# Parking all three merge gates in DRAM, running branch C ahead of branch A, and doing every convolution tap on VectorE

## The chip, the cores and the metric

The kernel runs on one core of one Trainium2 chip. The metric is the device time of one execution in microseconds (us), as the median of several runs.

## What is computed

Two decoder layers run over a prompt of 512 tokens and a sample group of 8 sequences with 4 new tokens each, 544 columns together. A layer projects the normalised input once and splits the result among three branches:

```python
u  = a_val * sigmoid(a_glu)                      # branch A: causal depthwise convolution, width 31
ya = silu(layernorm(conv31(u) + b_dw)) * silu(a_gate)
yb = sparse_attention(q, k, v, top-k of relu indexer) * silu(b_gate)   # branch B, prompt and paged cache
o, S = hgrn2(silu(cq), log_f, kk, ci, S0)        # branch C: gated linear recurrence
yc = rmsnorm(o) * silu(c_gate)
m = sigmoid(g_a)*(ya @ w_proj_a) + sigmoid(g_b)*(yb @ w_proj_b) + sigmoid(g_c)*(yc @ w_proj_c)
y = x + gate * (m @ w_out)
```

## The kernel before

Activations lie with channels on the 128 partitions and the 544 columns along the free dimension. Every projection is made of **products** (`product`, L493): one 128-column weight tile against all 544 columns. The weight is split into a rounded part `whi` (ScalarE) and a remainder `wlo` (VectorE, or GpSimd for every third product outside branch B's input), and three matmuls per 128 rows and column half (`whi` with `hhi`, `whi` with `hlo`, `wlo` with `hhi`) sum up in a PSUM tile `wide`, of which there are two. A product over 1024 rows has 48 matmuls of 272 columns, one over 512 rows (`projs`, names `yhi`, `ylo`) has 24. A layer has 73 of the first kind and 24 of the second.

Everything else is spread between the products. `spawn(gen, n, time)` registers a generator of n steps over `time` (a product over 1024 rows counts 5600 of it), `pump` runs due steps after each product, `drain` runs the rest. The program order and the priorities (`at`) feed a scheduler that writes one fixed instruction order for each engine; each engine then works its list in order and waits on semaphores. Loads and stores of one kind go through SyncE's queue (SP), the cache gathers through GpSimd's.

The order of a layer before, in products: branch B's inputs (9; called stage B below), first half of branch A (4, A0), first half of branch C (6, C0), second half of A (4, A1), second half of C (6, C1), the gates `gc` (8), `agate` (4), four times two `ga` gates and two of branch A's output projection (16, of them 8 short), `cgate` (4), C's output projection (8 short, PC), `gb` (8), `bgate` (4), B's output projection (8 short, PB), `w_out` (8). Beside them run:

- `sample_scores` (L921): keys are gathered, transposed (`gI` to `kit`), and 32 matmuls with an output of 32 partitions each (`hold<-kit,qib`) make the scores of one of four chunks. They stand in one block per chunk, 256 matmuls in all.
- `sample_select` (L966): a bit search in 31 steps; in each VectorE counts (`junk`), TensorE sums (`hold<-cnt`), VectorE decides (`rej`, `X`).
- `convolve` (L1205): per 128 channels 31 taps over 512 columns. The first 19 are VectorE's (one `tensor_scalar`, 18 `scalar_tensor_tensor`, `y<-u,wdw,y`, L1234). The other 12 (`CP`) are multiplied on ScalarE (`ctap`) and summed on GpSimd (`cpool`, L1239), and VectorE adds the two sums.
- the heads of branch C (`heads` in `branch_c`, on all engines), and `attends` (L876): prompt index with 16 rounds of `max` and `match_replace` for each of three query blocks (`prompt_masks`), sample attention, prompt attention.

Of the gates, `gc` is stored to DRAM (`gates`) and loaded back into a `th` tile, of which there are three, when C's projection needs it; `ga` goes to `th` tiles just ahead of its use, `gb` to eight tiles in SBUF.

Of the kernel before, what the change touches and what calls it, by code (L numbers as in the profile page):

```python
# [15 lines left out]
KD = D // 128  # L16
# [13 lines left out]
CP = 12  # L30
# [88 lines left out]
class _Kernel:  # L119
# [448 lines left out]
    def run(self):  # L568
# [33 lines left out]
        for l in range(self.depth):  # L602
# [15 lines left out]
            self.open("y")  # L618
            self.open("a", side="right")
# [4 lines left out]
            y = self.t([128, 4, NT], "y", "y")  # L624
            st = {}
            self.branch_a(l, h, V, y, 0, st)
# [5 lines left out]
            self.open("c")  # L632
            yc = self.t([128, 4, NT], "yy", "yc")
            self.branch_c(l, h, V, 0, yc, st)
# [4 lines left out]
            def gate_tile(f):  # L639
                return self.t([128, NT], "th", "w", bufs=3)  # L640
            self.gates("gc", h, gate_tile, then=lambda f, t: self.store(gd[:, f], t))
            self.drain(st["a0"], st["a1"], select)
            self.close("sel", "sidx", "a")
            self.open("split", side="right")
            ys = self.gated(COL["agate"], h, y, 0.5)
            m, mn, ta = [], [], {}

            def half():

                mn.append("m%d" % len(m))  # L650
                self.open(mn[-1], side="right")
                t = self.t([128, KD // 2, NT], "m", mn[-1])
                m.extend(t[:, f] for f in range(KD // 2))
            half()
            self.drain(st["c0"], st["c1"])
            self.close("c")
            half()
            self.open("isc")
            yb = [self.t([128, 4, NT], "y", "y")]
            attend = self.spawn(self.attends(l, r, yb), 75, 120000)  # L660

            def use_a(f, p):
                self.stt(self.two(m[f]), self.two(ta[f]), 1.0, p, OP.add, OP.mult)
            for f in range(0, KD, 2):
                self.gates("ga", h, gate_tile, range(f, f + 2), ta.__setitem__)
                self.projs(l, "w_proj_a", ys, range(f, f + 2), use_a)
            ys = self.gated(COL["cgate"], h, yc, 1.0)

            def use_c(f, p):
                t = self.t([128, NT], "th", "w", bufs=3)  # L670
                self.at(self.clk - 15000)
                self.load(t, gd[:, f], chain=False)
                self.at(self.clk - 16000)
                self.stt(self.two(t), self.two(t), 1.0, p, OP.add, OP.mult)
                self.tt(m[f], m[f], t, OP.add, eng=nc.gpsimd)
            tb = [self.t([128, 4, NT], "yy", "yc")]
            self.projs(l, "w_proj_c", ys, range(KD), use_c)
            self.open("tb")
            tb.append(self.t([128, 4, NT], "tb", "tb"))
            self.gates("gb", h, lambda f: tb[f // 4][:, f % 4])  # L680
# [4 lines left out]
            def use_b(f, p):  # L685
                t = tb[f // 4][:, f % 4]
# [4 lines left out]
            self.close("tb", "isc", "yc", "y", "keep")  # L691
            self.open("x")
            xT, w = self.out_proj(l, mh, xd, mod["g"], more)
            self.close(mn[1], mn[0], "split")
# [59 lines left out]
    def branch_b_in(self, l, h, V):  # L754
# [56 lines left out]
        scores = self.spawn(self.sample_scores(l, r), 9, 22500)  # L811
# [109 lines left out]
    def sample_scores(self, l, r):  # L921
# [9 lines left out]
        for c in range(4):  # L931
            sp = self.hold()
            kt = {}
            for hf in range(2):
                raw = next(raws)
                for rp in range(2):
                    b = self.bank()
                    for x in range(4):
                        self.tr(b[:, x * 128:(x + 1) * 128], raw[x][:, 2 * rp:2 * rp + 2].rearrange("p r d -> p (r d)"))
# [651 lines left out]
```

## Time and profile before

| | |
|---|---|
| median of 3 runs | 1712.63 us (1702.94 to 1713.41) |
| the profiled execution | 1704.63 us, span of its instructions 1702.8 us |
| TensorE matmul busy | 1567.7 us, 92% |
| VectorE, ScalarE, GpSimd busy | 1062.3 us (62%), 712.4 us (42%), 646.4 us (38%) |
| granted TensorE clock, mean | 0.950 |

TensorE is busy nearly all the time, and the share says little on how much of that time was needed: the clock and the idle time differ by stage. The stages of both layers therefore have to be read one by one, with the busy time of the other engines beside TensorE's.

### The profile page before, as it was taken

Reading aid. Unit: us, or ns where it says so; the run is one execution under the profiler, and the core shown is the slowest. Engines: PE = TensorE matmul, PEld = TensorE weight load, DVE = VectorE, ACT = ScalarE, POOL = GpSimd, SP = SyncE. Lnnn points to the kernel's source line nnn. Section 1 sums busy time; section 2 is a strip of 40 time slices with the busy share of each in tenths; the row PEclk is TensorE's granted clock in tenths of the full one; section 3 lists DMA queues with packets and bytes.
Section 4 is the critical chain, followed back from the end, with each engine's and each line's share of the span. In section 5 each row is a group of like instructions: output and inputs, shape, how many; then the busy total and the mean of one; then the engine's idle time right before and its main releaser. Section 6 shows DMA issues by size and latency. Waiting matters only on the chain.

```text
span 1702.8 us, 31340 instructions
## 1 busy us (share of the span) xinstructions
PE 1567.7 (92%) x12580; PEld 1412.2 (83%) x12580; DVE 1062.3 (62%) x2047; ACT 712.4 (42%) x1205; POOL 646.4 (38%) x536
## 2 busy tenths in 40 slices
PE   8889879889999999999988897878999999999998
PEld 5677778789998788998887687878899888799998
DVE  4433898987848474345555149899886485543562
ACT  4345443455354242453233455325633433334432
POOL 0332575574524544110321316674643444431010
PEclk9989989899999999999988898989999999999999
DMA  9653521232354556315725342212323655552131
GB/s 357 217 161 109 199 54 59 75 90 85 107 150 150 153 180 179 88 50 198 267 96 160 92 121 67 73 50 76 103 82 102 187 142 164 169 136 84 50 134 47
DMA packets 95209, 215.49 MB, mean 127 GB/s; under 512 B 11949, under 2 KB 41363, under 8 KB 94024
## 3 DMA queue, kind: packets, MB, share of 16 engines
q1 hardware_dynamic: 81752, 171.53, 32.4%
q0 software_dynamic: 13312, 41.96, 8.3%
q8 instruction: 99, 1.62, 0.4%
q14 instruction: 46, 0.38, 0.1%
HBM read 183.90 MB, written 26.22 MB: 123 GB/s over the span
## 4 chain that ended last, share of the span: by engine, by line
PE 66%; DVE 17%; issue 7%; DMA 4%; ACT 2%; POOL 1%; another core or an unknown queue 1%; SPq 0%; ACTq 0%; DVEq 0%; POOLq 0%
PE wide L197 46%; PE bk L197 8%; DVE y L228 7%; PE hold L197 7%; PE bk L201 5%; DVE wlo L220 2%; DVE hE L220 1%; DMA araw<-in_w_ada 1%; DVE y L225 1%; DVE junk L225 1%; DVE hqa L220 1%; DVE X L228 1%; DMA xraw<-in_constf 1%; DMA wraw<-in_w_in 1%
## 5 line engine op out<-in xcount | busy, mean ns | idle before, releaser
L197 PE MATMUL wide<-hhi,whi 128*128 128x272 f32 (+1 forms) x2336 | 523.6, 302 | 32.1 <-DVE ht L225 9.1
L197 PE MATMUL wide<-hhi,wlo 128*128 128x272 f32 (+1 forms) x2336 | 524.2, 302 | 11.6 <-DVE wlo L220 8.4
L197 PE MATMUL wide<-hlo,whi 128*128 128x272 f32 (+1 forms) x2336 | 524.3, 302 | 1.2 <-issue 1.0
L197 PEld LDWEIGHTS wide<-hhi,whi 128*128 128x128 f32 (+1 forms) x2336 | 387.3, 196 | 47.5 <-issue 32.3
L197 PEld LDWEIGHTS wide<-hhi,wlo 128*128 128x128 f32 (+1 forms) x2336 | 386.8, 196 | 24.4 <-issue 12.9
L197 PEld LDWEIGHTS wide<-hlo,whi 128*128 128x128 f32 (+1 forms) x2336 | 387.0, 196 | 13.6 <-issue 11.0
L209 ACT ACTIVATE whi<-wraw 128x1024 fp32r<-128x1024 f32 (+2 forms) x198 | 183.7, 931 | 315.7 <-PE wide L197 226.9
L220 POOL TENSOR_TENSOR wlo<-wraw,whi 128x1024 fp32r<-128x1024 f32 (+1 forms) x58 | 123.1, 2123 | 447.2 <-ACT whi L209 387.4
L220 DVE TENSOR_TENSOR wlo<-wraw,whi 128x1024 fp32r<-128x1024 f32 (+2 forms) x140 | 160.3, 1146 | 127.8 <-ACT whi L209 101.7
L220 POOL TENSOR_TENSOR cpool<-cpool,ctap 128x512 f32<-128x512 f32 (+1 forms) x94 | 142.1, 1512 | 56.9 <-ACT ctap L209 41.2
L228 DVE SCALAR_TENSOR_TENSOR y<-u,wdw,y 128x512 f32<-128x512 f32 x144 | 159.1, 1118 | 0.4
L916 POOL DMA_INDIRECT gI<-in_cache_idx_k,idx x64 | 64.2, 1003 | 129.9 <-PE bk L201 111.9
L916 POOL DMA_INDIRECT gKV<-in_cache_v,idx x64 | 63.1, 985 | 80.0 <-PE bk L201 32.6
L209 ACT ACTIVATE ctap<-u,wdw 128x512 f32<-128x512 f32 x88 | 62.7, 719 | 69.9 <-POOL cpool L220 69.8
L197 PE MATMUL wide<-yhi,whi 128*128 128x272 f32 x384 | 84.5, 297 | 7.6 <-DVE gate L228 3.2
L916 POOL DMA_INDIRECT gKV<-in_cache_k,idx x64 | 65.3, 1020 | 61.3 <-PE bk L201 28.0
L197 PE MATMUL wide<-yhi,wlo 128*128 128x272 f32 x384 | 82.3, 293 | 0.8 <-issue 0.8
L197 PE MATMUL wide<-ylo,whi 128*128 128x272 f32 x384 | 82.7, 293 | 0.0
L209 ACT ACTIVATE kt<-bk 128x512 f32<-128x512 f32 x80 | 46.4, 596 | 81.5 <-PE hold L197 29.9
L197 PEld LDWEIGHTS wide<-yhi,whi 128*128 128x128 f32 x384 | 61.8, 192 | 12.2 <-ACT whi L209 5.6
L197 PE MATMUL bk<-hqa,hk 128*128 128x64 f32 (+2 forms) x480 | 62.1, 263 | 4.0 <-DVE hqa L220 3.9
L238 DVE CUSTOM_DVE_ANT_0 P<-bk,isc 128x512 f32<-128x512 f32 (+2 forms) x48 | 25.5, 556 | 63.5 <-PE bk L197 63.4
(334 smaller groups left out, 2444.3 us busy)
## 6 DMA issues: line engine op xcount, KB each, us to landing
wraw<-in_w_in SPq DMA_DIRECT2D x128, 512.0 KB
wraw<-in_w_ada SPq DMA_DIRECT2D x32, 512.0 KB
araw<-in_w_ada SPq DMA_DIRECT2D x16, 512.0 KB
wraw<-in_w_out SPq DMA_DIRECT2D x16, 512.0 KB
xpark<-xT SPq DMA_DIRECT2D x4, 1088.0 KB
gates<-th SPq DMA_DIRECT2D x16, 272.0 KB
th<-gates SPq DMA_DIRECT2D x16, 272.0 KB
xT<-xpark SPq DMA_DIRECT2D x4, 1088.0 KB
```

The source lines that it names most:

```text
L197: return self.tick(self.nc.tensor.matmul(out, lhsT, rhs, start=start, stop=stop))
L201: self.tick(self.nc.tensor.transpose(out, in_, self.ident[b:b + n, b:b + n]))
L209: i = self.nc.scalar.activation(out, in_, f, **k)
L220: self.tick((eng or self.nc.vector).tensor_tensor(out, a, b, op=op))
L225: self.tick((eng or self.nc.vector).tensor_scalar(out, a, s1, s2, op0=op0, **k))
L228: self.tick(self.nc.vector.scalar_tensor_tensor(out, a, s, b, op0=op0, op1=op1))
L238: self.tick(getattr(self.nc.vector, f)(*a, **k))
L916: self.tick(self.chain("gather", self.nc.gpsimd.indirect_dma_start(out=raw, out_offset=None, in_=rows, in_offset=bass.IndirectOffsetOnAxis ...
```

## The change

- The gate products move: `gc` directly behind branch B's inputs, `ga` and `gb` behind both halves of A. All three are stored to DRAM and loaded back one tile at a time (`parked`), eight loads in each of the three output projections.
- Branch C (12 products) comes ahead of branch A (8).
- The new order of a layer: B (9), `gc` (8), C0 (6), C1 (6), A0 (4), A1 (4), `ga` (8), `gb` (8), `agate` (4), A's projection (8 short, PA), `cgate` (4), PC (8 short), `bgate` (4), PB (8 short), `w_out` (8).
- The scores of the sample keys are spread over 60000 in place of 22500, and the matmuls of a chunk come in two halves, each one step behind its transposes.
- The convolution is drained after the gates and not before `agate`; attention starts with `ga` and has 175000 in place of 120000.
- All 31 taps are VectorE's but the first, which is ScalarE's; `cpool` and `ctap` go.

```diff
             r, scores = self.branch_b_in(l, h, V)
...
+            def park_gates(name):
+                g = gd[name] = self.tc.dram_tile([128, KD, NT], F32, name="%s%d" % (name, l))
+                self.gates(name, h, lambda f: self.t([128, NT], "th", "w", bufs=3),
+                           then=lambda f, t: self.store(g[:, f], t))
+
+            def parked(name, f):
+                t = self.t([128, NT], "th", "w", bufs=3)
+                self.at(self.clk - 15000)
+                self.load(t, gd[name][:, f], chain=False)
+                self.at(self.clk - 16000)
+                return t
+            park_gates("gc")
             self.drain(scores)
...
             select = self.spawn(self.sample_select(l, r), 36, 70000)
...
             self.branch_c(l, h, V, 0, yc, st)
+            self.branch_c(l, h, V, 1, yc, st)
...
+            self.branch_a(l, h, V, y, 0, st)
             self.branch_a(l, h, V, y, 1, st)
-            self.branch_c(l, h, V, 1, yc, st)
-            gd = self.tc.dram_tile([128, KD, NT], F32, name="gates%d" % l)
...
-            self.drain(st["a0"], st["a1"], select)
+            self.drain(st["c0"], st["c1"], select)
...
+            attend = self.spawn(self.attends(l, r, yb), 75, 175000)
+            park_gates("ga")
+            park_gates("gb")
+            self.drain(st["a0"], st["a1"])
...
             def use_a(f, p):
-                self.stt(self.two(m[f]), self.two(ta[f]), 1.0, p, OP.add, OP.mult)
+                t = parked("ga", f)
+                self.stt(self.two(m[f]), self.two(t), 1.0, p, OP.add, OP.mult)
+            self.projs(l, "w_proj_a", ys, range(KD), use_a)
...
             def use_b(f, p):
-                t = tb[f // 4][:, f % 4]
+                t = parked("gb", f)
                 self.stt(self.two(t), self.two(t), 1.0, p, OP.add, OP.mult)
...
-        scores = self.spawn(self.sample_scores(l, r), 9, 22500)
+        scores = self.spawn(self.sample_scores(l, r), 9, 60000)
...
-        z = self.t([128, NT], "cpool", "a")[:, :TP]
-        self.tsc(yp, u[:, 0:TP], w[:, 0:1], V["bdw"][:, f:f + 1], OP.mult, OP.add)
-        self.act(z, u[:, 31 - CP:31 - CP + TP], AF.Copy, scale=w[:, 31 - CP:32 - CP])
-        for k in range(max(CP - 1, 30 - CP)):
-            if k < 30 - CP:
-                self.stt(yp, u[:, k + 1:k + 1 + TP], w[:, k + 1:k + 2], yp, OP.mult, OP.add)
-            if k < CP - 1:
-                n = 32 - CP + k
-                x = self.t([128, NT], "ctap", "a", bufs=2)[:, :TP]
-                self.act(x, u[:, n:n + TP], AF.Copy, scale=w[:, n:n + 1])
-                self.tt(z, z, x, OP.add, eng=gp)
+        self.act(yp, u[:, 0:TP], AF.Identity, scale=w[:, 0:1], bias=V["bdw"][:, f:f + 1])
+        for k in range(1, 31):
+            self.stt(yp, u[:, k:k + TP], w[:, k:k + 1], yp, OP.mult, OP.add)
             if k % 3 == 2:
                 yield
-        self.tt(yp, yp, z, OP.add)
```

On VectorE, in the second half of branch C in layer 0, taps stood before among the heads' work (`hE`, `hqa`), the select's count (`junk`) and the splits:

```order
L228 SCALAR_TENSOR_TENSOR y<-u,wdw,y 128x512
L225 TENSOR_SCALAR junk,cnt_2017<-isc_s,X 128x544
L220 TENSOR_TENSOR hqa<-hqa,hE_3021 128x8x32
L228 SCALAR_TENSOR_TENSOR y<-u,wdw,y 128x512
L220 TENSOR_TENSOR hE_4030<-hE_4004 128x136
```

Now they stand mostly in the gates `ga` and `gb` of layer 0, among the prompt index (`isc`) and the splits:

```order
L219 TENSOR_TENSOR wlo_456<-wraw,whi_455 128x1024
L227 SCALAR_TENSOR_TENSOR y<-u,wdw,y 128x512 x6
L224 TENSOR_SCALAR isc_4417<-irel,wi 128x256
L227 SCALAR_TENSOR_TENSOR y<-u,wdw,y 128x512 x2
L237 TENSOR_REDUCE y<-cprod 128x16
L234 COPY us<-u 128x8x4
L227 SCALAR_TENSOR_TENSOR isc_4417<-irel,wi,isc_4417 128x256
L219 TENSOR_TENSOR wlo_458<-wraw,whi_457 128x1024
```

The taps moved from the heads of branch C to the start of attention.

On TensorE, in branch B's inputs of layer 0, the first scores of the sample keys (`hold`) were one block before:

```order
L197 MATMUL wide<-hhi,whi_463 128x272 x2
L197 MATMUL wide<-hlo,whi_463 128x272
L197 MATMUL hold<-kit,qib 32x128 x32
L197 MATMUL wide<-hlo,whi_463 128x272
L197 MATMUL wide<-hhi,wlo_464 128x272 x2
```

Now each of them stands between matmuls of a product:

```order
L196 MATMUL hold_919<-kit_910,qib_451 32x128
L196 MATMUL wide_1047<-hlo_363,whi0_455 128x272
L196 MATMUL hold_919<-kit_910,qib_451 32x128
L196 MATMUL wide_1047<-hhi_362,wlo0_456 128x272
L196 MATMUL hold_919<-kit_910,qib_451 32x128
L196 MATMUL wide_1047<-hhi_362,wlo0_456 128x272
L196 MATMUL hold_919<-kit_910,qib_451 32x128
L196 MATMUL wide_1047<-hhi_362,whi0_455 128x272
```

Of the 256 such matmuls of the program 24 were followed at once by one of a product, now 251 are.

On SyncE's queue, around B's projection in layer 0, only weights stood before:

```order
L244 DMA wraw<-in_w_proj_b 128x1024 x2
L244 DMA wraw<-in_w_ada 128x1024 x4
L244 DMA wraw<-in_w_proj_b 128x1024 x2
L244 DMA wraw<-in_w_ada 128x1024 x4
L244 DMA wraw<-in_w_out 128x1024 x2
```

Now the loads of the parked `gb` stand between them:

```order
L243 DMA wraw<-in_w_proj_b 128x1024 x2
L243 DMA th<-gb_5376 128x544 x2
L243 DMA wraw<-in_w_ada 128x1024
L243 DMA th<-gb_5376 128x544
L243 DMA wraw<-in_w_ada 128x1024 x3
L243 DMA wraw<-in_w_proj_b 128x1024
L243 DMA xT<-xpark 128x2176 x2
L243 DMA wraw<-in_w_proj_b 128x1024
```

A load that waits for its `th` tile now stands ahead of weights in the same queue.

## Rows read from the trace of the kernel before

**Rows 1.** The page, part 1: busy time, share of the span, instructions.

```profile
PE 1567.7 (92%) x12580; PEld 1412.2 (83%) x12580; DVE 1062.3 (62%) x2047; ACT 712.4 (42%) x1205; POOL 646.4 (38%) x536
```

**Rows 2.** Windows by stage: layer 0 B, C0 to gc; layer 1 the same.

```profile
core 0: us, PE busy (x) PEld busy (x) DVE busy (x) ACT busy (x) POOL busy (x), PEclk, DMA share, GB/s
30.40:150.30 119.90, 107.63 (x777) 82.68 (x776) 47.52 (x95) 44.32 (x75) 38.83 (x43) 0.91 0.59 197
...
188.00:441.30 253.30, 219.91 (x1611) 209.70 (x1612) 229.77 (x389) 110.86 (x176) 151.23 (x112) 0.91 0.27 81
...
877.80:993.40 115.60, 101.44 (x727) 83.37 (x728) 44.37 (x78) 44.77 (x74) 27.83 (x31) 0.83 0.34 101
...
1023.90:1274.20 250.30, 214.52 (x1596) 204.34 (x1595) 227.12 (x384) 113.76 (x178) 150.61 (x113) 0.92 0.25 73
```

**Rows 3.** Windows, columns as in rows 2: C1, and `ga` with A's projection, layer 0.

```profile
292.00:362.70 70.70, 58.45 (x403) 55.87 (x403) 69.46 (x105) 31.06 (x51) 43.28 (x34) 0.85 0.23 68
...
474.80:595.90 121.10, 115.82 (x1053) 101.93 (x1052) 68.40 (x158) 51.78 (x84) 53.66 (x49) 0.99 0.52 153
```

**Rows 4.** The chain that ended last: start us, length us, what.

```profile
838.53 15.03 PE wide L197 x119
```

**Rows 5.** Groups of instructions: count, busy us, mean ns, idle before, releaser.

```profile
L220 DVE TENSOR_TENSOR wlo<-wraw,whi 128x1024 fp32r<-128x1024 f32 (+2 forms) x140 | 160.3, 1146 | 127.8 <-ACT whi L209 101.7 <-remote 11.6 <-issue 10.5
L228 DVE SCALAR_TENSOR_TENSOR y<-u,wdw,y 128x512 f32<-128x512 f32 x144 | 159.1, 1118 | 0.4
L220 POOL TENSOR_TENSOR cpool<-cpool,ctap 128x512 f32<-128x512 f32 (+1 forms) x94 | 142.1, 1512 | 56.9 <-ACT ctap L209 41.2 <-ACT cpool L209 11.8 <-POOL cpool L220 0.3
...
L197 PE MATMUL bk<-hqa,hk 128*128 128x64 f32 (+2 forms) x480 | 62.1, 263 | 4.0 <-DVE hqa L220 3.9
...
L238 DVE MAX8 m<-isc 128x8 f32<-128x256 f32 (+2 forms) x96 | 53.7, 559 | 2.3
L238 DVE MATCH_REPLACE8 isc<-m,isc 128x256 f32<-128x256 f32 (+2 forms) x96 | 52.1, 542 | 0.0
...
L197 PE MATMUL hold<-kt,qbd 128*32 128x128 f32 x512 | 23.5, 281 | 0.5 <-issue 0.5
```

**Rows 6.** Instructions on tile wdw: count, ns min/median/max, first and last start.

```profile
L228 DVE SCALAR_TENSOR_TENSOR y<-u,wdw,y x144: 733/741/6350, 180.6 to 1199.5; 128x512 f32<-128x512 f32 x144
```

**Rows 7.** Instructions on tile kit: idle before them, us and times, by releaser.

```profile
  issue: 48.0, 72
```

**Rows 8.** Timeline of PE: narrow and wide matmuls by turns, in layer 1.

```profile
932.53 0.59 PE L197 MATMUL wide<-hhi,whi 128*128 128x272 f32 x1
933.05 0.64 PE L197 MATMUL hold<-kit,qib 128*32 128x128 f32 x2
933.62 0.60 PE L197 MATMUL wide<-hlo,whi 128*128 128x272 f32 x1
...
1478.30 0.29 PE L197 MATMUL wide<-yhi,wlo 128*128 128x272 f32 x1
1478.52 0.30 PE L197 MATMUL hold<-gKV,kt 128*32 128x128 f32 x1
1479.25 0.29 PE L197 MATMUL hold<-gKV,kt 128*32 128x128 f32 x1 [0.43 <-issue]
1479.47 0.39 PE L197 MATMUL wide<-yhi,wlo 128*128 128x272 f32 x1
```

**Rows 9.** Windows, columns as in rows 2: PC of layer 0; around the turns of layer 1.

```profile
634.30:670.30 36.00, 31.97 (x271) 29.00 (x270) 13.62 (x21) 8.43 (x15) 18.94 (x16) 0.95 0.72 204
...
925.00:950.00 25.00, 21.01 (x94) 13.76 (x93) 3.55 (x5) 5.57 (x8) 4.31 (x5) 0.66 0.32 102
```

**Rows 10.** Waits of SyncE's queue: waited for, us in total, times, longest us.

```profile
SPq L244 <- POOL m L220: 34.5, 8, 13.5
```

More of the change, by code (lines that the diff above doesn't have):

```diff
@@ L29 @@
 WB = 6
-CP = 12
 HK = 4
@@ L631, in run @@
             self.open("yc")
-            self.open("c")
+            self.open("c", side="right")
             yc = self.t([128, 4, NT], "yy", "yc")
+            st = {}
             self.branch_c(l, h, V, 0, yc, st)
-            self.branch_a(l, h, V, y, 1, st)
-            self.branch_c(l, h, V, 1, yc, st)
-            gd = self.tc.dram_tile([128, KD, NT], F32, name="gates%d" % l)
-            def gate_tile(f):
-                return self.t([128, NT], "th", "w", bufs=3)
-            self.gates("gc", h, gate_tile, then=lambda f, t: self.store(gd[:, f], t))
@@ L656, in run @@
[L656 to L660, printed above, removed]
+            self.branch_c(l, h, V, 1, yc, st)
+            self.open("y")
+            self.open("a")
+            y = self.t([128, 4, NT], "y", "y")
+            self.branch_a(l, h, V, y, 0, st)
+            self.branch_a(l, h, V, y, 1, st)
+            self.drain(st["c0"], st["c1"], select)
+            self.close("c", "sel", "sidx")
@@ L662, in use_a @@
+            m = [t[:, f] for t in ms for f in range(KD // 2)]
             def use_a(f, p):
-                self.stt(self.two(m[f]), self.two(ta[f]), 1.0, p, OP.add, OP.mult)
-            for f in range(0, KD, 2):
-                self.gates("ga", h, gate_tile, range(f, f + 2), ta.__setitem__)
-                self.projs(l, "w_proj_a", ys, range(f, f + 2), use_a)
+                t = parked("ga", f)
+                self.stt(self.two(m[f]), self.two(t), 1.0, p, OP.add, OP.mult)
+            self.projs(l, "w_proj_a", ys, range(KD), use_a)
@@ L667, in run @@
             ys = self.gated(COL["cgate"], h, yc, 1.0)
             def use_c(f, p):
[L670 to L673, printed above, removed]
+                t = parked("gc", f)
                 self.stt(self.two(t), self.two(t), 1.0, p, OP.add, OP.mult)
                 self.tt(m[f], m[f], t, OP.add, eng=nc.gpsimd)
-            tb = [self.t([128, 4, NT], "yy", "yc")]
@@ L930, in sample_scores, with part @@
         raws = self.ahead(gathers())
[L931 to L939, printed above, removed]
-                    kt[rp, hf] = self.t([128, 4, 128], "kit", "sg", bufs=4)
-                    self.cp(kt[rp, hf], b.rearrange("p (x k) -> p x k", x=4))
-                yield
+        def part(c, hf, kt, sp):
             for r4 in range(4):
@@ L945, in sample_scores @@
                 for b2 in range(2):
-                    for pr in range(4):
+                    for pr in (2 * hf, 2 * hf + 1):
                         self.mm(sp[32 * pr:32 * pr + 32, k], qib[:, r4 % 2, 2 * pr + b2],
-                                kt[r4 // 2, pr // 2][:, 2 * (pr % 2) + b2], start=b2 == 0, stop=b2 == 1)
+                                kt[r4 // 2][:, 2 * (pr % 2) + b2], start=b2 == 0, stop=b2 == 1)
+            if hf == 0:
+                return
             R = self.t([128, 512], "irel_s", "sg", bufs=2)
@@ L954, in sample_scores @@
             self.cp(sc[s, :512], b[s])
+        last = None
+        for c in range(4):
+            for hf in range(2):
+                raw = next(raws)
+                kt = []
+                for rp in range(2):
+                    b = self.bank()
+                    for x in range(4):
+                        self.tr(b[:, x * 128:(x + 1) * 128], raw[x][:, 2 * rp:2 * rp + 2].rearrange("p r d -> p (r d)"))
+                    kt.append(self.t([128, 4, 128], "kit", "sg", bufs=4))
+                    self.cp(kt[rp], b.rearrange("p (x k) -> p x k", x=4))
+                if last:
+                    part(*last)
+                if hf == 0:
+                    sp = self.hold()
+                last = (c, hf, kt, sp)
+                yield
+        part(*last)
         b = self.bank()
@@ L1284, in heads @@
                 yield
-        st["c%d" % h2] = self.spawn(heads(), 14, (40000 if h2 == 0 else 44000))
+        st["c%d" % h2] = self.spawn(heads(), 14, (34000 if h2 == 0 else 44000))
     def head_in(self, n, hh, st, p, V):
```

47 lines of the change are left out of this document (18 added, 29 removed).

## Prediction

> **What bounds the kernel now.** I read the page's busy shares first, then the stages by windows, then the groups of instructions in the stage that loses most. TensorE is busy for 92% of the span [rows 1], but busy time contains slow clock and matmuls that wait inside, so I measure each stage against what its matmuls need. A wide matmul in an undisturbed run starts every 15.03 / 119 = 0.126 us [rows 4], so a product of 48 needs 6.05 us. For the other matmuls I take 0.09 us a record, between the 62.1 / 480 = 0.13 of `bk<-hqa,hk` and the 23.5 / 512 = 0.05 of `hold<-kt,qbd` [rows 5]; this is an estimate.
>
> From C0 to `gc` there are 28 products, 169.3 us. The windows count 1611 and 1596 records there [rows 2]; 1344 are the products', so 267 and 252 others cost 24 and 23 us. The need is 193 and 192 us, the stages last 253.3 and 250.3: 60 and 58 us are lost in the two layers. In the same rows VectorE is busy for 229.8 and 227.1 us, 91%, and in C1 for 69.46 of 70.70 us [rows 3], where TensorE's granted clock has a mean of 0.85. So VectorE sets the pace of these stages and TensorE waits, partly idle, partly at its lower level. Elsewhere VectorE is not the limit: in `ga` with A's projection it is busy for 68.4 of 121.1 us, TensorE for 115.8 [rows 3].
>
> What fills VectorE there is taps: 144 at a mean of 1118 ns, though the median is 741 and the longest 6350 [rows 5, 6]. GpSimd's `cpool`, 94 times 1512 ns [rows 5], runs in the same stretches; the gap between mean and median is the price of that company.
>
> **The change part by part.** Sums are made against the profiled execution, 1704.6 us (span 1702.8). The median of the three runs is 1712.6, 0.5% above it; about 1% is what a measurement of this kernel can tell from no change.
>
> *Branch C's stages lose their taps.* In the new order `gc`, C0 and C1 hold 165 VectorE instructions in layer 0 and no tap. Before, the 389 instructions of C0 to `gc` [rows 2] had 72 taps, 80 us; the rest averages 150 / 317 = 0.47 us, so 165 cost 78 us. TensorE needs 20 x 6.05 = 121 us for the products and, with 304 other matmuls of two records each, 55 us: 176 us, more than twice VectorE's. The 118 us lost before should go: **-118**; with the other records at 0.13 or 0.05 it is -96 or -141. I leave in these stages what a stage with a slack VectorE still loses, 5.3 of 121.1 us or 4.4% [rows 3], on 2 x 176 us: **+15**.
>
> *The taps go to A0, A1, `ga`, `gb`.* All 30 per group are VectorE's now, 240 in place of 144. Per layer 120 taps at 0.77 us make 92 us. I take 0.77 since `cpool` is gone and the quiet tap is 0.741; the far end is 1.118 [rows 5, 6]. Then 16 splits at 1.146 = 18 us; 26 (layer 0) and 31 (layer 1) pairs of `max` and `match_replace` at 0.559 + 0.542 = 29 and 34 us [rows 5]; and 160 other instructions. Without taps, splits and pairs VectorE has 637 us in 1571 instructions [rows 1, 5], 0.41 us each, so 65 us. The sum is 204 and 210 us. TensorE needs 24 x 6.05 = 145 us and, for 348 and 388 other matmuls of two records, 63 and 70: 208 and 215. The two engines are level, and level is not free. If VectorE reaches the 91% of rows 2, the stages last 225 and 231 us: 17 and 16 us lost, **+33**. The lower bound is the 4.4% of a slack stage, +18; the upper has taps at 1.118, which adds 42 us of VectorE per layer, gives 271 and 278 us, and loses 126.
>
> ScalarE loses 88 multiplications and GpSimd 88 sums. Both are worth nothing by themselves (42% and 38% busy, rows 1); their worth is the tap's price, counted above.
>
> *Parked gates.* `ga` and `gb` add 32 stores and 32 loads. The stores follow a gate product that nothing waits for, beside other work: 0. The loads stand on SP's queue ahead of weights, and each waits until one of three `th` tiles is free. Before, SP waited for GpSimd's sum `m` in exactly these loads of `gc`, 8 times and 34.5 us in all, 13.5 at the longest [rows 10]. What of it reached TensorE is seen in PC of layer 0: 36.0 us, of which 8 short products need 192 x 0.126 = 24.2 and 79 others 7.1 [rows 9]; 4.7 us lost, 0.6 per load. In PA and PB no `m` sum on GpSimd holds the tile, VectorE frees it directly, so I take half, 0.3 x 32 = **+10** (0 to +19). Queued behind a waiting load are weights of PA, PB, PC and `w_ada`; they are needed some products later.
>
> *Key scores.* Their 256 matmuls of 32 output partitions stood in blocks of 32, and their tile lists 48.0 us of idle with no releaser, in 72 pieces [rows 7]; at 0.05 us a record the work itself is another 23 us, 71 in all. Now 251 of them stand singly between wide matmuls. At full clock the step wide to narrow takes 0.22 us (1478.30 to 1478.52) and narrow to wide 0.22 (1479.25 to 1479.47) [rows 8]. A pair is 0.44 in place of 0.126, 0.31 more: 251 x 0.31 = 78 us. The spread pays about as much as it gets back: 0, with bounds of -30 (these stages also ran at 0.91 and 0.83 of the clock, rows 2) and +25. The Trainium skill, "TensorEngine Tiling (Array Packing)", speaks against this edit: it says that a change of tiling mode drains TensorE. The two steps of 0.22 us in place of 0.126 agree. By that rule alone, with 470 more changes of tile size at 0.09 us and nothing of the idle given back, the sum would end 44 us higher, at 1689.
>
> The other moves (attention started earlier, A's inputs later, `u` tiles from two to four) have their instructions in the counts above.
>
> **Sum:** 1704.6 - 118 + 15 + 33 + 10 = 1645 us, and its own range by the bounds above, without the far end of the taps, 1605 to 1685.
>
> **The rivals.**
>
> (1) *Slower: taps stay at 1.118 us.* Splits, `hk`, `cprod` and gathers are still GpSimd's and can keep VectorE company in A0 to `gb`. Then the excess is 126 and not 33: 1738 us. It passes 1705 when a tap takes about 1.0 us. Against it: GpSimd's busy time falls by over 130 us with `cpool`, and the median was 741 ns even before. Chance 6%. The page "SBUF — State Buffer" of the Trainium skill, "Who interferes with whom", has the mechanism: a VectorE instruction with two SBUF inputs and a GpSimd instruction that reads SBUF exclude each other for a whole instruction.
>
> (2) *Slower: turns of narrow and wide at the lower clock.* Around 925 to 950 us of before such turns ran at a granted clock of 0.66 [rows 9], and a pair took 1.09 us (932.53 to 933.62, rows 8), at the 1.2 GHz level. If all 251 do so, 251 x 0.65 = +163: 1808 us. From 92 pairs on the kernel is slower. For it: in the new order few matmuls of these stages stand in long rows of one size. Against: the old stretch was also starved, with 21.0 of 25.0 us busy in 94 records. Chance 8%.
>
> (3) *No change: the heads' own chain, not VectorE's load, costs C0 and C1.* C1 of layer 0 needs 36.3 + 115 x 0.09 = 46.7 us and lasts 70.7 [rows 3]: 24 lost, in C0 by the same count about 22, so 92 in both layers would stay. 1704.6 - 118 + 92 + 33 + 10 = 1722 us. Against it: VectorE had 1.2 us of idle in C1, and `bk<-hqa,hk` waited for `hqa` for only 4.0 us [rows 5]. Chance 11%.
>
> (4) *Better: level is free after all.* With deep enough spreading the excess of 33 and the rest of 15 vanish: 1597 us. Chance 13%.
>
> **How the numbers follow.** The forecast has 62%, the rivals 6, 8, 11 and 13. The range goes from 1600 to 1710: it holds the forecast's own, half of (4) and a share of (3), and leaves out (1), (2) and most of the rest. Faster by over 1%: the forecast without a small upper tail, and (4), 74%. Within 1%: (3) and that tail, 15%. Slower: (1), (2) and the upper part of (3), 11%.
>
> **What the profile after would show.** Right: the tap's mean falls from 1118 to about 770; from `gc` to C1 TensorE is near 176 us per layer at full clock; A0 to `gb` is some 225 to 230 us with VectorE at 90%; the three short projections lose about 0.3 us per load; the idle before `hold<-kit,qib` shrinks, while its pairs take 0.44 us. Wrong: taps over 1.0 us, a granted clock near 0.5 in B and `gc`, C0 and C1 still over 55 us each, or SP waiting for `th` with TensorE idle behind it. The forecast fails most easily at the A stages, where a tenth more work for VectorE costs 20 us per layer, and at the key scores, where two sums of 70 us cancel.

## The result and the profile after

The changed kernel takes 1768.88 us (median of 4 runs, 1766.5 to 1770.37), the kernel before 1708.64 us beside it: a ratio of 1.0353 (95% interval 1.0311 to 1.0395). It is 3.5% slower; 1645 us and a gain were forecast, with a range up to 1710.

The stages show at once where the time went and where it did not. These are windows of the kernel after, columns as in [rows 2]: for layer 0 stage B, `gc`, C0 with C1, A0 to `gb`, `agate`, A's projection; for layer 1 `gc`, A0 to `gb`, `agate`.

```profile
31.70:146.00 114.30, 109.53 (x655) 77.72 (x656) 50.73 (x99) 40.10 (x70) 31.15 (x34) 0.99 0.59 197
146.00:256.40 110.40, 110.40 (x664) 74.79 (x663) 13.85 (x25) 29.58 (x46) 17.03 (x19) 0.95 0.40 126
256.40:366.70 110.30, 103.27 (x816) 99.48 (x815) 76.09 (x191) 42.65 (x64) 37.62 (x34) 0.95 0.28 81
366.70:589.10 222.40, 208.86 (x1709) 196.42 (x1708) 196.41 (x360) 83.47 (x135) 92.76 (x69) 0.98 0.41 123
589.10:662.70 73.60, 59.69 (x561) 46.05 (x560) 48.50 (x103) 31.11 (x54) 41.00 (x36) 0.91 0.49 142
662.70:710.30 47.60, 38.31 (x363) 34.95 (x362) 21.63 (x44) 13.60 (x23) 10.28 (x11) 0.89 0.64 180
...
1023.40:1123.80 100.40, 100.40 (x617) 69.88 (x616) 12.39 (x20) 28.32 (x44) 17.85 (x19) 1.00 0.32 99
...
1232.90:1457.70 224.80, 212.13 (x1781) 199.81 (x1780) 199.61 (x373) 84.81 (x138) 102.13 (x72) 0.98 0.41 123
1457.70:1531.70 74.00, 59.78 (x488) 44.98 (x487) 46.13 (x93) 30.09 (x49) 36.71 (x35) 0.82 0.47 136
```

Three readings. A0 to `gb` take 222.4 and 224.8 us; 225 and 231 were forecast, and VectorE is busy for 196 and 200 us of them. The taps' new place costs what it was said to. But `gc`, whose products need 48 us, takes 110.4 and 100.4 us with TensorE busy without a gap at nearly full clock: no wait shows, so the cost sits in the matmuls themselves. And `agate` takes 73.6 and 74.0 us, with 14 us of idle time in each and a clock of 0.91 and 0.82. Before, it took 33.5 and 31.6 us:

```profile
441.30:474.80 33.50, 33.50 (x284) 32.43 (x283) 22.62 (x35) 12.30 (x25) 12.81 (x9) 1.00 0.41 121
1274.20:1305.80 31.60, 31.56 (x269) 30.59 (x268) 25.95 (x40) 11.34 (x23) 13.36 (x11) 1.00 0.39 117
```

Part of that is work that moved there: 561 and 488 matmul records stand in place of 284 and 269, which at the prediction's estimate of 0.09 us a record is 25 and 20 us.

For `gc`, the timeline of TensorE in the kernel after: start, length, what.

```profile
181.04 0.41 PE L196 MATMUL hold<-kit,qib 128*32 128x128 f32 x2
181.38 0.39 PE L196 MATMUL wide<-hlo,whi 128*128 128x272 f32 x1
181.69 0.41 PE L196 MATMUL hold<-kit,qib 128*32 128x128 f32 x2
182.03 0.39 PE L196 MATMUL wide<-hhi,wlo 128*128 128x272 f32 x1
```

Beside it the weight loads of the same stretch:

```profile
181.37 0.19 PEld L196 LDWEIGHTS wide<-hlo,whi 128*128 128x128 f32 x1 [0.20 <-issue]
181.69 0.14 PEld L196 LDWEIGHTS hold<-kit,qib 128*32 128x32 f32 x2
182.03 0.19 PEld L196 LDWEIGHTS wide<-hhi,wlo 128*128 128x128 f32 x1 [0.20 <-issue]
```

From one key-score matmul (two records) to the next it is 0.65 us (181.04 to 181.69): 0.34 us until the wide matmul starts and 0.31 until the next narrow one. The wide matmul's weights are loaded 0.33 us after the narrow matmul's start, behind 0.20 us in which no weights are loaded; in [rows 4] a wide matmul starts every 0.126 us. A turn so costs 0.53 us above a wide matmul (the median over the trace is 0.656 us from wide to wide across a turn), not the 0.31 forecast, and the busy share cannot show it, because the records fill the time. The 251 turns make 133 us; the group `hold<-kit,qib` shows no idle time of its own.

Is it the narrow tile, or would any small f32 matmul of two records cost that? The same trace has such matmuls on the whole array (`128*128`) between wide ones, in C1:

```profile
307.19 0.38 PE L196 MATMUL bk<-hq,hk 128*128 128x128 f32 x2
307.32 0.37 PE L196 MATMUL wide<-hhi,wlo 128*128 128x272 f32 x1
307.54 0.38 PE L196 MATMUL bk<-hq,hk 128*128 128x128 f32 x2
```

There a turn takes 0.35 us (307.19 to 307.54), so 0.22 of the 0.53 us go with a matmul of this size, and the other 0.31 with the narrow tile.

For `agate`, the chain that ended last, in layer 0, start, length, what:

```profile
630.47 1.63 PE hold L196 x9
632.18 0.60 ACT kt L208
632.78 0.55 ACT u L208
633.40 0.52 POOL u L219
633.92 0.86 issue
634.82 1.33 POOL u L219
636.23 1.34 POOL u L219
637.62 2.09 PE bk L196 x2
...
642.60 2.87 DVE y L227 x4
645.47 0.66 DVE isc L237 x2
646.13 0.61 DVE S L224 x2
646.74 1.24 DVE y L224 x3
```

TensorE's own work ends the chain no longer. From 632 us it goes through ScalarE, GpSimd and VectorE: the layer norm (`u`, `y`) behind the last tap, with attention's `isc` and `S` between its steps. The products of `agate` have their two PSUM tiles full, since `gate` has one buffer and is read only with the normed `y`. On VectorE the first product's `gate` is written at 608.10 and the second's only at 654.07; on TensorE no wide matmul starts between the two below:

```profile
608.10 0.71 DVE L227 SCALAR_TENSOR_TENSOR gate<-th,wide 128x544 f32<-128x544 f32 x1
654.07 0.70 DVE L227 SCALAR_TENSOR_TENSOR gate<-th,wide 128x544 f32<-128x544 f32 x1
```

```profile
622.83 0.42 PE L196 MATMUL wide<-hhi,wlo 128*128 128x272 f32 x2
655.17 0.52 PE L196 MATMUL wide<-hhi,whi 128*128 128x272 f32 x2
```

The forecast had no term for that. The change also stretched the convolution's steps, from 34000 and 58000 to 56000 and 85000, which the list of its parts does not name; that places the layer norm later still.

### The profile page after: what moved, and what is told of

It reads as the page before. It is cut to its first block, busy times and chain, and to the rows that moved or that the text cites. A ratio compares the mean times of both kernels' runs of the same rounds, so it can differ in the third digit from the quotient of the medians.

```text
span 1767.8 us, 31347 instructions
## 1 busy us (share of the span) xinstructions
PE 1654.0 (94%) x12580; PEld 1420.1 (80%) x12580; DVE 1034.2 (59%) x2127; ACT 653.6 (37%) x1113; POOL 533.5 (30%) x448
## 4 chain that ended last, share of the span: by engine, by line
PE 71%; DVE 14%; issue 6%; DMA 3%; POOL 2%; ACT 2%; another core or an unknown queue 1%; SPq 0%; ACTq 0%; POOLq 0%; DVEq 0%
PE wide L196 48%; PE bk L196 9%; PE hold L196 9%; DVE y L227 6%; PE bk L200 5%; DVE wlo L219 1%; DMA gKV<-in_cache_k,idx 1%; DVE hqa L219 1%; DVE isc L237 1%; DVE hE L219 1%; DVE att L237 1%; DMA hs<-in_state_hgrn 1%; DVE m L237 1%; POOL wlo L219 0%
## 5 line engine op out<-in xcount | busy, mean ns | idle before, releaser
L196 PE MATMUL wide<-hlo,whi 128*128 128x272 f32 (+1 forms) x2336 | 530.9, 301 | 1.7 <-issue 1.4
L196 PEld LDWEIGHTS wide<-hhi,whi 128*128 128x128 f32 (+1 forms) x2336 | 379.1, 191 | 38.9 <-issue 25.6
L196 PEld LDWEIGHTS wide<-hlo,whi 128*128 128x128 f32 (+1 forms) x2336 | 380.4, 191 | 33.9 <-issue 31.2
L196 PEld LDWEIGHTS wide<-hhi,wlo 128*128 128x128 f32 (+1 forms) x2336 | 378.2, 191 | 31.2 <-issue 27.9
L219 POOL TENSOR_TENSOR wlo<-wraw,whi 128x1024 fp32r<-128x1024 f32 (+1 forms) x58 | 129.7, 2237 | 544.5 <-ACT whi L208 526.5
L219 DVE TENSOR_TENSOR wlo<-wraw,whi 128x1024 fp32r<-128x1024 f32 (+2 forms) x140 | 154.0, 1103 | 176.2 <-ACT whi L208 163.9
L227 DVE SCALAR_TENSOR_TENSOR y<-u,wdw,y 128x512 f32<-128x512 f32 x240 | 200.9, 884 | 0.0
L196 PE MATMUL hold<-kit,qib 128*32 128x128 f32 x512 | 105.5, 288 | 0.0
L196 PEld LDWEIGHTS wide<-yhi,wlo 128*128 128x128 f32 x384 | 61.6, 192 | 4.1 <-issue 3.7
L196 PEld LDWEIGHTS hold<-kit,qib 128*32 128x32 f32 x512 | 35.4, 108 | 35.7 <-issue 3.6
```

The source lines that it names most:

```text
L196: return self.tick(self.nc.tensor.matmul(out, lhsT, rhs, start=start, stop=stop))
L219: self.tick((eng or self.nc.vector).tensor_tensor(out, a, b, op=op))
L227: self.tick(self.nc.vector.scalar_tensor_tensor(out, a, s, b, op0=op0, op1=op1))
```

## Experiments

The runs fell on chips of two speeds: the kernel before takes 1709, 1708 and 1697 us on the slower ones (the first comparison and two of the groups below) and 1632 to 1633 us on the quicker ones. Times are compared with the kernel before on the same chip, as ratios.

**Key scores as before, in the new order.** `sample_scores` from the kernel before, and

```diff
-        scores = self.spawn(self.sample_scores(l, r), 9, 60000)
+        scores = self.spawn(self.sample_scores(l, r), 9, 22500)
```

> The kernel after with one thing undone: the sample key scores are written as before (one block of 32 matmuls per chunk, spread over 22500). Theory K (the turns of narrow and wide matmuls made the change slower): in the trace of after a pair of one wide matmul and one key-score matmul takes 0.65 us at full clock where a wide one alone takes 0.126, so 251 turns cost 131 us, against some 70 us that the blocks and their idle time cost before. Undone, the kernel takes about 1769 - 61 = 1708 us (1695 to 1720). Rival L (the late layer norm alone made it slower): the time stays within 10 us of 1769. If the turns cost as little as the prediction had it, 0.44 us a pair, it also stays within 10 us.

1706.77 us, 0.9984 of before (0.9957 to 1.0011). This one edit takes the whole loss back, 62 us.

**Key scores spread as in after, but in rows.** One line at the head of `part`:

```diff
+            self.at(self.clk - 200)
```

> The kernel after, with the key scores still spread over 60000 and still in halves one step behind their transposes, but each half's 16 matmuls have an earlier place in the order, so that they stand in rows of 8 or 16 on TensorE and not singly between wide matmuls. Theory K: it is the turns that cost, not the spreading. 251 turns at 0.52 us above a wide matmul become some 20 changes and 512 records at 0.05 us (23 us): 1769 - 131 + 33 = about 1670 us (1655 to 1690). Rival (a spread that leaves TensorE waiting for transposes and copies costs, however the matmuls stand): not below 1740. Rival L: within 10 us of 1769.

1677.49 us, 0.980 (0.9754 to 0.9847): the turns as such cost, not the spreading. The timeline of TensorE in this kernel has the same 16 matmuls in one row:

```profile
103.98 0.41 PE L196 MATMUL wide<-hhi,wlo 128*128 128x272 f32 x2
104.32 1.94 PE L196 MATMUL hold<-kit,qib 128*32 128x128 f32 x32
106.19 0.52 PE L196 MATMUL wide<-hhi,whi 128*128 128x272 f32 x2
```

That is 1.87 us from 104.32 to 106.19, 0.12 us a matmul in place of 0.53. And the blocks of before were dear as well on these chips. The 48.0 us in [rows 7] are not all TensorE's idle time, though: they add up two groups that wait in the same stalls, matmuls and weight loads.

```profile
L197 PE MATMUL hold<-kit,qib 128*32 128x128 f32 x512 | 36.3, 309 | 17.7 <-issue 16.7 <-ACT qr L209 1.0
L197 PEld LDWEIGHTS hold<-kit,qib 128*32 128x32 f32 x512 | 19.7, 120 | 33.2 <-issue 31.4 <-ACT qr L209 1.3
```

The matmuls' part, 16.7 us, is 19.6 with the blocks in the new order and nothing with the rows. Read from start to start (from the last other matmul before a group to the next one behind it, less 0.126 us), the key scores hold TensorE for 136 us in after, 61 with the blocks and 33 with the rows.

**Attention behind the gates, convolution earlier.**

```diff
-            attend = self.spawn(self.attends(l, r, yb), 75, 175000)   # ahead of ga
+            attend = self.spawn(self.attends(l, r, yb), 75, 130000)   # ahead of agate
-        ... (56000 if f2 == 0 else 85000)
+        ... (42000 if f2 == 0 else 62000)
```

> The kernel after with the convolution's steps over 42000 and 62000 in place of 56000 and 85000, and with attention started behind the gates (over 130000) and not with the gates, so that the convolution and its layer norm are through before agate. Theory L: agate with A's projection takes 121 and 115 us in after, where their products and other matmuls need about 97 and 90 by the same count; that falls, and the kernel takes about 1769 - 45 = 1724 us (1710 to 1745). What stays slow is the key scores. Rival (the pieces of attention that now come later crowd the projections instead): within 10 us of 1769. Theory K alone says no change here either.

1773.35 us, 1.038 (1.0326 to 1.0434), no gain. Windows of this kernel, `agate` and `bgate` of layer 0:

```profile
563.80:598.40 34.60, 34.60 (x308) 31.27 (x307) 28.66 (x59) 20.19 (x33) 10.36 (x9) 1.00 0.41 121
739.00:830.90 91.90, 76.48 (x581) 58.85 (x580) 43.76 (x147) 42.22 (x108) 6.22 (x4) 0.93 0.35 95
```

`agate` is back at 34.6 us, and `bgate` (42.2 us in after) takes 91.9: the rest of attention is drained there. The time of `agate` fell as the theory said, but this cure moved it, as the rival said. The run changes two things at once: with 308 matmul records in `agate` in place of 561, it does not separate the wait for the layer norm from attention's work in that stage.

**Taps shared out as before, in the new order** (`CP = 12`, `cpool` and `ctap` back, `u` in two tiles).

> The kernel after with the taps shared out as before (12 of 31 on ScalarE and GpSimd, cpool and ctap back, two u tiles as before); the order of the layer stays. By the prediction's term, 120 taps per layer at 0.77 us (92 us) become 72 at about 1.12 (81 us) plus 8 sums: VectorE's work in A0 to gb hardly changes, GpSimd and ScalarE get 88 operations back: 1769 give or take 10 us. Theory L's rival form (VectorE alone with the taps is what makes the convolution late): 1740 or less. If cpool still delays taps in this order and the sums come later still: 1780 to 1800.

1808.85 us, 1.0578 (1.0529 to 1.0626): 40 us slower than after. The expectation of no change was wrong; its last case, 1780 to 1800, came nearest. The window of A1 in layer 0:

```profile
398.10:470.70 72.60, 51.32 (x355) 47.25 (x353) 69.81 (x92) 21.18 (x39) 53.63 (x40) 0.77 0.19 58
```

It is 38.4 us long in after. VectorE is full again beside a GpSimd busy for 54 of 73 us, and the mean of 144 taps is 1124 ns, as in [rows 5]. So the taps' part of the change is a gain by itself. That GpSimd's company makes the difference, the starts and ends in the trace of before bear out: the 55 taps that overlap a `cpool` sum take 1.57 us on average, the 58 that overlap nothing on GpSimd 0.74.

**VectorE's taps alone, in the order of before.**

> The kernel before with one part of the change alone: all taps but the first are VectorE's, cpool and ctap go; the order of the layer, the gates and the key scores stay. Theory T (GpSimd's company is what made taps dear): 240 taps at 0.74 us in place of 144 at 1.118 add 18 us of VectorE, but the other VectorE work of C0 to gc gets quicker too; from the 40 us that the same part is worth in the order of after (1808.9 against 1768.9), the time is about 1708 - 35 = 1673 us (1655 to 1695). Rival (VectorE is the bound there and only the number of its instructions counts): 8 x 11 more taps in a stage that is already VectorE's make it slower, 1720 to 1745. Rival (the taps are off the path in this order): within 10 us of 1708.

On a quicker chip 1602.8 against 1632.9 us, 0.9813 (0.9791 to 0.9836): a gain of 1.9% without any new order. VectorE has 80 instructions more (2127 against 2047) and the kernel is quicker: without `cpool`, C0 to `gc` of layer 0 hold 380 VectorE instructions and 203 us of its time in the repeated run below, against 389 and 229.8 in [rows 2], which come from a slower chip.

**Scores in rows, in the order of before; and both.** The edits above.

> The kernel before with the key scores alone changed: spread over 60000, in halves one step behind their transposes, each half's matmuls in rows of 8 or 16 (no turns with wide matmuls). Theory K: the blocks of before waited for their transposes and copies (48 us of idle on that tile); in the order of after rows are worth 1706.8 - 1677.5 = 29 us against the blocks. Here about 1708 - 29 = 1679 us (1665 to 1695). Rival (what is given back in branch B's inputs is lost in A0, where the rest of the scores falls): 1700 to 1715.

> The kernel before with both: scores in rows as in the run above and all taps on VectorE, in the layer order of before. If the two parts add, 1708 - 29 - 35 = about 1644 us (1625 to 1665), and against after with rows (1677.5) this says what the new order of the layer with three parked gates costs by itself: some 33 us. Rival (the new order is what pays for VectorE's taps, as the prediction had it): 1680 or more.

1637.91 us, 1.0031 (1.0017 to 1.0044), and 1599.31 us, 0.9802 (0.9786 to 0.9818), on the same quicker chip. Rows gain nothing there. The reason is in the kernels with blocks: in the run with VectorE's taps alone, on this chip, the idle time on `kit` is 4.8 us in 7 pieces, all of it weight loads', and not 48.0 in 72, for the same code; the matmuls wait for nothing. What rows give back was lost on the slower chips alone. A saving taken over from one chip to another was my mistake in these two expectations. The taps' gain shows here on one chip: C0 to `gc` of layer 0 take 254.6 us with rows and the taps of before, 225.6 with rows and VectorE's.

**The convolution's steps earlier, with rows.**

> The kernel after with scores in rows (1677.5 us) and the convolution's steps over 42000 and 62000 in place of 56000 and 85000, attention as in after. Theory L2 (agate waits for the layer norm because its steps are placed last): agate and A's projection of 124 and 119 us fall by 20 us per layer: about 1640 us. Rival (VectorE has no room in A1 to gb, it is busy for 88 to 100% there, so earlier steps only displace the prompt's max and match_replace into the later stages, as in the run with late attention): 1670 to 1685.

1628.65 us, 0.9971 (0.9958 to 0.9983). The run fell on a quicker chip, so neither expected time can be compared; rows alone take 1645.15 us on another quicker chip (next group), 16.5 us more. But `agate` with A's projection falls by 5 and 4 us only, from 109.0 and 103.5 to 104.2 and 99.6, and not by 20 per layer.

**The kernel after, two variants and VectorE's taps alone, on one quicker chip.**

> The kernel after once more, beside three others on one chip, since the kernel before took 1707.7 us on the chip of the first four runs and 1632.9 on that of the next four, where the idle time before key scores without a releaser is 4.8 and not 48.0 us. Theory K: the turns cost 131 us on any chip (they run at full clock with no idle), while the blocks of before cost their 48 us of idle only where that idle shows. On the slower chip the ratio to before is 1.035 again; on the quicker one the change looks worse, about 1.06 (1725 to 1745 us). Rival (all stages scale alike): 1.035 on both.

> The kernel after with the key scores of before (blocks, 22500). On the slower chip 1707 us again. On the quicker one the blocks are not starved and blocks and rows are about level: 1640 us (1625 to 1655), some 95 below after.

> The kernel after with the scores in rows. On the slower chip 1677 again; on the quicker one within 8 us of the run with blocks, as in the order of before, where rows gave a ratio of 1.003.

> The kernel before with all taps but the first on VectorE, beside the kernel after with the key scores of before: these two have the same taps and the same scores and differ in the order of the layer and the parked gates alone. Theory O (the new order costs, since agate and A's projection then wait for the layer norm): this one is 30 to 45 us faster on either chip (1603 against 1640, or some 1670 against 1707). Rival (the prediction's: the order is what pays): it is slower than the other by 20 us or more. Rival (order and gates are worth nothing either way): within 10 us.

After: 1743.82 us, 1.0674 (1.0647 to 1.0701). Blocks: 1635.87, 1.0020 (1.0007 to 1.0033). Rows: 1645.15, 1.009 (1.006 to 1.0119). VectorE's taps in the old order: 1604.0, 0.9822 (0.9799 to 0.9845). Three came as expected; rows lie 9 us above blocks, where at most 8 was said. The turns cost 108 us against blocks where blocks are not starved and 62 where they are. Read from start to start, the blocks hold TensorE for 25 us here and the turns for 133: a difference of 108. On the slower chip the same count gives 136 - 61 = 75, of which other stages take some back. And with taps and scores alike the rest of the change (new order, parked gates, the other placing of convolution and attention) makes the kernel 32 us slower.

**Half the turns.** In `part`, with `p0` the place at its start and `n` a counter:

```diff
+                        self.at(p0 + 4 * (n // 4))
```

> The kernel after with the key scores' places in the order set in fours, which leaves 129 groups of 1 to 4 between wide matmuls in place of 251 single ones; all else as in after. Theory K by dose: after is 98.7 us (1743.8 - 1645.2) above rows on the quicker chip and 91.4 (1768.9 - 1677.5) on the slower. Half the turns should cost half of it: some 1692 us on the quicker chip, 1723 on the slower (give or take 12). Rival (it is the spreading under wide matmuls as such, whatever the group): no change against after.

1720.33 us on a slower chip, 1.012 (1.0072 to 1.0167), where 1723 was expected: on the slower chips of the earlier runs after has 1.0353 and rows 0.980. Neither of the two ran on this chip, so the place of this run between them is by ratios alone. Read from start to start, the key scores hold TensorE for 74 us here, for 136 in after and 33 in rows: the cost goes roughly by the number of groups.

**Parked loads twice.**

```diff
                 self.load(t, gd[name][:, f], chain=False)
+                self.load(t, gd[name][:, f], chain=False)
```

> The kernel after with scores in rows, and each of the 48 loads of parked gates issued twice into the same tile. If a parked load costs what the prediction took, 0.3 us each for 32 of them, 48 more cost 14 us (1659 on the quicker chip, 1692 on the slower); at the upper bound of 0.6, 29 us. If the loads are hidden, no change from rows (1645 or 1677) by more than 5 us.

1684.96 us, 0.9925 (0.990 to 0.995) against rows' 0.980: 21 us, 0.4 us for each of 48. This is no clean price: rows did not run on this chip, the second load must wait for the first, and SP's waits for landings of `th` add up to 64 us here against 4 with single loads.

**The layer norm ahead in line.** Besides the earlier convolution, in `layer_norm` at each step:

```diff
+        self.at(self.clk - 12000)
```

> The kernel after with scores in rows and the convolution's steps over 42000 and 62000: again 0.997 of before on the quicker chip (1628 us); on the slower, where rows give 0.98, 1677 - 16 = about 1661. It is here to be compared with the next run on the same chip.

> The run above, with the layer norm of branch A also placed 12000 earlier in the priorities (two products' worth), so that its steps on VectorE, GpSimd and ScalarE stand ahead of the prompt's max and match_replace and of the gathers. Theory L2 (what is left of the wait of agate and A's projection is the layer norm's chain standing in line with attention's work): agate of 64 and 62 us falls by 10 or more in each layer, and the whole by 15 to 25 us. Rival (the chain itself, with its sums on GpSimd, two means over TensorE and its table loads, takes that long however it is placed): within 6 us.

1655.94 us, 0.9753 (0.9712 to 0.9794), and 1639.8 us, 0.9667 (0.9623 to 0.9712), on one slower chip: 16 us. In layer 0 `agate` hardly falls, from 67.6 to 64.3 us, where 10 or more was expected. `agate` and A's projection of layer 1, first without and then with the layer norm ahead:

```profile
1341.60:1406.20 64.60, 52.82 (x443) 42.08 (x442) 34.51 (x67) 28.27 (x47) 36.30 (x31) 0.89 0.49 144
1406.20:1451.80 45.60, 40.27 (x393) 34.55 (x392) 25.84 (x53) 12.14 (x20) 13.96 (x14) 0.93 0.56 175
```

```profile
1339.10:1388.50 49.40, 44.41 (x365) 36.60 (x364) 25.78 (x50) 22.65 (x37) 32.23 (x28) 0.93 0.57 170
1388.50:1429.60 41.10, 38.11 (x399) 33.64 (x397) 31.08 (x68) 14.75 (x24) 17.48 (x18) 0.97 0.61 190
```

**The best of both orders, on one quicker chip.**

> The order of before with scores in rows and VectorE's taps, against the best of the new order on one chip. On the quicker chip 0.980 of before again; on the slower, where rows are worth more, about 0.955. Theory O (the new order as such costs): it is at least 8 us faster than the next run. Rival (the new order cost only by where the convolution and its layer norm stood): within 6 us, or slower.

> The new order with scores in rows, the convolution's steps earlier and the layer norm ahead in line: 0.967 of before on the slower chip again, on the quicker about 0.988 (0.997 less 16 us).

1601.08 us, 0.9799 (0.9782 to 0.9815), against 1627.18, 0.995 (0.9932 to 0.9969). The layer norm's place gives next to nothing here (0.9971 without it, on another quicker chip), where 16 us were expected, and the new order stays 26 us behind the old one with the same taps and scores. The fastest version on the quicker chips is the order of before with VectorE's taps, with or without rows; on a slower chip it did not run.

## Why the prediction was wrong

The miss of 124 us (1768.9 against 1645) falls into two halves. With the key scores of before, the term that the sum put at 0, the kernel takes 1706.8 us: 62 us are the key scores, and the other 62 are the rest of the sum.

**The step that failed: key scores at 0.** Its one half was nearly right. The blocks' price of 71 us (48.0 of idle and 23 of work) counts the idle time of matmuls and of weight loads for the same stalls; from start to start the blocks hold TensorE for 61 us. That 133 - 71 is just the 62 us measured is luck. The other half was wrong: "a pair is 0.44 in place of 0.126" came from [rows 8], where one record of the narrow matmul stands on either side of an idle gap, and the sum left out what lies between. A key-score matmul has two records, which do not overlap with the wide ones on either side, and a turn takes 0.656 us: 133 us where 78 stood in the sum. The trace of before had such turns whole, in 13 places at full clock with a median of 0.55 us, one of them here (the second wide matmul of the first line starts at 572.62):

```profile
572.50 0.41 PE L197 MATMUL wide<-hhi,wlo 128*128 128x272 f32 x2
572.84 0.41 PE L197 MATMUL hold<-gKV,kt 128*32 128x128 f32 x2
573.17 0.39 PE L197 MATMUL wide<-hhi,whi 128*128 128x272 f32 x1
```

In the half-clock rows of [rows 8] the pair was there too with both its records, 1.09 us; half of that is 0.55. Rival (2) had the mechanism (turns, one by one), but tied it to the lower clock and priced it by that: 163 us above the sum's 78, where the turns cost 55 above them, at full clock. The bounds of -30 to +25 took nothing of this in. The drain that the Trainium skill states ("TensorEngine Tiling (Array Packing)", Key Properties) agrees with these rows, and it costs more than the 0.09 us per change by which I weighed it: a turn has two changes and takes 0.31 us more than the same turn on the whole array.

**The step that was missing: agate.** The sum followed the taps to A0 to `gb` and stopped there. With the key scores of before, the stages that it priced, `gc` to `gb`, take 792 us in both layers, some 30 less than the 823 forecast. The loss is behind them. `agate` of that run, columns as in [rows 2]:

```profile
551.90:626.50 74.60, 58.83 (x488) 44.71 (x487) 46.43 (x93) 30.50 (x50) 36.10 (x34) 0.84 0.47 135
1391.00:1465.40 74.40, 59.47 (x488) 45.03 (x487) 45.74 (x92) 30.10 (x49) 36.59 (x35) 0.82 0.46 135
```

That is 149 us against 65 before. By the estimate of 0.09 us a record, 38 of the 84 are matmuls that moved there, and 46 are lost. What comes after the last tap, two column means with their sums on GpSimd, a table load and sixteen VectorE steps, stood before under eight `gc` products; now it stands at the drain just ahead of `agate`, and one `gate` buffer passes the wait on to TensorE. Earlier convolution and layer norm in line, against rows alone, give back 18 us on the quicker chips and some 23 (0.980 to 0.9667, ratios from two chips) on the slower ones, so part of this half is shown by experiment; what would give back the rest stays open.

With rows and both repairs the kernel is at 0.967 on a slower chip, where 0.963 was forecast. That closeness is luck as well: rows save 29 us against the blocks there, which the sum did not count on, and on a quicker chip the same kernel is at 0.995.

**Point by point.** *Branch C's stages*: with blocks, so nearly without the turns, `gc`, C0 and C1 take 175 and 164 us; 183 was forecast (176 and a rest). The 118 us did go from these stages. *Taps in A0 to `gb`*: right in length (above); the tap's mean was not 0.77 but 0.884 us (240 taps, 200.9 us in the kernel after; median 739 ns), which other work made up for: VectorE was busy for 196 and 200 us where 204 and 210 were summed up. Rival (1) did not come. *GpSimd's and ScalarE's 88 operations at nothing*: their worth, counted in the tap's price, is 40 us in the new order (a slower chip) and 28 to 30 in the old one (quicker chips). *Parked gates at +10*: in after, `th<-th,wide` and `m<-th,wide` together wait 1.8 us for landings, so single loads cost next to nothing; the doubled ones only bound it. *Rival (3)*, the heads' own chain, fell in the main. C0 and C1 of after take 110.3 us in layer 0 where 131.2 went before. C1 alone still takes 69 us in each layer, over the 55 that the prediction named as a sign of being wrong; but it holds 515 and 513 matmul records where [rows 3] has 403, and by the prediction's own count 12 to 13 us are lost in it, not 24.

**Where the expected gain went.** The order of the layer frees branch C's stages and gives the time away later. Windows of layer 0, before: B to `gc`, `agate` with `ga` and A's projection, `gb`; then the new order with the key scores of before: B to A1, `ga` to A's projection.

```profile
30.40:441.30 410.90, 365.23 (x2730) 323.91 (x2729) 299.82 (x514) 179.66 (x288) 198.94 (x164) 0.92 0.39 124
441.30:595.90 154.60, 149.32 (x1335) 134.35 (x1334) 91.02 (x193) 64.08 (x107) 66.47 (x58) 0.99 0.50 146
670.30:744.10 73.80, 73.80 (x597) 68.21 (x596) 30.00 (x99) 34.37 (x79) 10.88 (x5) 1.00 0.29 82
```

```profile
30.10:399.70 369.60, 344.96 (x2715) 307.62 (x2714) 205.21 (x442) 140.06 (x220) 112.19 (x107) 0.96 0.42 135
399.70:674.20 274.50, 237.31 (x2046) 208.65 (x2045) 206.40 (x378) 102.00 (x170) 114.05 (x95) 0.92 0.52 154
```

The first part is 41 us shorter and the second 46 longer; in layer 1 it is 45 and 32, and the stages behind take 10 us more in both layers together. VectorE's taps by themselves leave C0 to `gc` at 218 us in the old order, on a quicker chip, and need no new one. The last 26 us between the two orders (rows and VectorE's taps in both) lie in the same stages: `ga`, `gb`, `agate` and A's projection take 25 and 23 us longer in the two layers of the new order, the stages ahead of them 9 and 6 less (the profiled runs lie 33 us apart). Which of the pieces that meet there (taps, layer norm, prompt index) holds TensorE up is not settled; no run separated them.

## What to carry to other kernels

A matmul of a narrow tile put singly between the long ones cost half a microsecond here that no idle time and no clock showed: read it from start to start across a whole turn, with all records of the odd matmul, and keep small matmuls in rows. Before two idle times are added up, see whether they belong to the same stall. When work is moved later, follow it to its last consumer, the layer norm and the gate here, and not only to the stage in which it runs. And of a bundle of edits try the smallest alone: on one chip VectorE's taps without the new order gained 1.8%, and the whole bundle lost 6.7%.

## What was not expected of the hardware

The same code for stage B leaves TensorE's matmuls idle without a releaser for 16.7 us before the key scores on one chip (its weight loads for 31.4) and not at all on another (4.8), and the kernel before takes 1708 and 1633 us there; what differs between the chips isn't shown by these traces. A narrow-tile matmul between wide ones takes 0.656 us from wide to wide, a whole-array matmul of the same type and number of records 0.35. And a VectorE tap gets cheaper by more than its own share when GpSimd's sums go: in the new order 96 more taps, without 94 sums and 88 ScalarE products beside them, made the kernel 40 us faster.
